# The S5 stage of a hybrid trunk kernel, put into a written order on all engines

## The chip, the cores and the metric

The kernel runs on one core of one Trainium2 chip. A core has TensorE (PE, with its weight loads PEld), VectorE (DVE), ScalarE (ACT), GpSimd (POOL) and SyncE (SP, which here only issues DMAs), each with a queue of its own that is worked off in order. The metric is the device time of one execution in microseconds (us), the median of several runs; lower is better.

## The reference

The input x has 512 tokens of 1024 channels, float32. Two layers follow each other; each is half a SwiGLU FFN (inner width 2816), a token mixer and another half FFN, all on RMS-normalised input with a residual. The first layer's mixer is a Mamba-2 SSD, the second's is an S5 diagonal state space model, and the change lies in that one:

```python
lam_bar = jnp.exp(lam * step)
b_bar = ((lam_bar - 1.0) / lam)[..., None] * lax.complex(b_re, b_im)
bu = jnp.einsum('bqgc,gpc->bqgp', uc.astype(jnp.complex64), b_bar)
...
_, states = lax.associative_scan(s5_binop, (a, bu), axis=1)   # state_t = lam_bar * state_(t-1) + bu_t
yc = jnp.einsum('gcp,bqgp->bqgc', c, states).real
...
y = jnp.moveaxis(ys, 0, 1).reshape(bsz, L, dm) + d * u
g = jax.nn.gelu(y)
val, gate = jnp.split(g @ glu_w + glu_b, 2, axis=-1)
return val * jax.nn.sigmoid(gate)
```

There are 64 groups of 16 channels with 64 complex states each. The GLU multiplies the 1024 channels by a 1024 x 2048 matrix.

## The kernel before, in words

The residual xT is held as eight tiles of 128 channels x 512 tokens. The kernel runs six stages: FFN, SSD, FFN, FFN, S5, FFN. Products are made with a high and a low half of each operand (three matmuls: hi x H, hi x L, lo x H; `proj`, lines 222 to 228). A weight tile is split by a cast on ACT (`whi`, line 217) and a subtraction on DVE (`wlo`, line 219). The FFN in front of S5 is `ffn7`; its last part writes the eight tiles of xT one after the other (line 587), stores each to DRAM as `d_u` (`s5_sink`, line 1289) and adds up the squares. A list `fill` of 62 small jobs is worked off beside it; jobs 54 to 61 come after the eight last columns.

**Layout of S5.** The 512 tokens are seen as 64 blocks of 8. u is read back from DRAM so that a partition holds one channel and one place in the block (`U`, 128 x 8 groups x 64 blocks, line 1316). Eight such tiles, i = 0 to 7, are worked on in pairs. For each i:

- U is multiplied by the norm factor rL (DVE, line 1368).
- 16 small matmuls with `opH` give the blocks' contributions to the states, `pb` (PE, line 1377).
- The scan over the 64 blocks, done in a turning frame so that the decay is real: two copies that swap the real and the imaginary half (ACT, lines 1380 and 1381), products with the table `tb` and their sum (DVE, lines 1382 to 1384), the scan itself (line 1386), two copies back (ACT, lines 1390 and 1391) and three DVE rows that turn the result into v (lines 1392 to 1394). The decay `rh` is laid out by POOL (lines 1370 and 1371).
- `mix`: for a pair and each half of its groups, eight matmuls on U and eight on v with `opP` (line 1404) and a gelu on ACT (line 1407).
- `channels`: transposes (line 1418) put a pair back into channels x tokens, and ACT and DVE split it into GH and GL (lines 1422 and 1423).
- `glu_k(k)`: the k-th of eight slices of the first four GLU column blocks (12 matmuls, lines 226 to 228). These four, `res`, have their weights split before the stage (lines 1346 and 1347). The fifth block, p0, gets 18 matmuls after glu_k(4) and glu_k(5), and six more after glu_k(7). The eleven others follow whole.

**The norm.** `compact_sum` (line 147) leaves the sum of squares of token t in a 128 x 4 layout, `newton_rsqrt` (lines 131 to 138) makes its inverse root in 13 small DVE rows, and lines 1355 to 1361 bring it into U's layout: a product with a mask, four matmuls with `sel` and a copy.

**What sets the order.** Under `manual_schedule(engines=MAN)` only PE keeps the order of the program text; a planner with a model of the times orders the other engines' work. Under `engines=ALL`, as inside `ffn7`, all five engines keep the order of the text. In before the S5 stage stands under MAN. Tiles come from pools with a fixed number of buffers: five for opH and tb together, five for opP, four for U, four PSUM banks for pb, mix and channels. A load into a buffer waits on SP until its last reader is done, and what SP has behind it waits too.

## Time and profile before

| | |
|---|---|
| median of 3 runs | 2068.3 us (2066.34 to 2068.41) |
| the profiled execution's own time | 2066.69 us |
| its span, first to last instruction | 2064.9 us |
| PE busy | 2005.0 us, 97% of the span |
| DVE, ACT, POOL busy | 1415.6, 890.3, 143.9 us |
| mean granted TensorE clock | 0.988 |

The S5 stage lies from about 1546 to 1706 us. In the profile's row of 40 slices for PE it is the one place (slice 31, from 1548.7 us) where the busy tenths fall to 5. An instruction's row in the timeline gives its start, its duration, engine, line, operation, tiles and shapes, "x" with the number of like instructions put together, and in brackets the idle time of the engine before it and what ended that. A float32 matmul counts as two (two passes), a split one as one.

### The profile page before, as it was taken

What the parts mean: (1) busy time and instruction counts of PE and PEld (TensorE: products, weight loads), DVE (VectorE), ACT (ScalarE), POOL (GpSimd) and SP (SyncE); (2) the same over time, 40 slices, a digit from 0 to 9 for tenths busy, and PEclk for the clock granted to TensorE, in tenths of its full rate; (3) what the DMA queues carried; (4) which work ended last, traced back from release to release, by engine and by line L of the source; (5) the groups of instructions that cost most, each with busy time, mean ns of one, the idle gap of its engine ahead of it and who ended that gap; (6) DMA issues with size and microseconds to landing.
All of it is one profiled execution on the core that took longest, in us unless ns stands there. A gap on an engine that the chain in (4) does not pass through costs nothing.

```text
span 2064.9 us, 30435 instructions
## 1 busy us (share of the span) xinstructions
PE 2005.0 (97%) x11905; PEld 1711.8 (83%) x11905; DVE 1415.6 (69%) x2494; ACT 890.3 (43%) x1454; POOL 143.9 (7%) x218
## 2 busy tenths in 40 slices
PE   8999999999999999999999999999995999999997
PEld 7888888878878877887788888999984888999996
DVE  6899445678875777557864567667667546866675
ACT  5322233556653674333433334444444433444553
POOL 1000000011110110000000000001111000100010
PEclk9999999999999999999999999999997999999999
DMA  6455643433334323535553325546769232755561
GB/s 168 113 147 161 173 112 86 117 113 100 108 106 110 107 69 112 160 101 160 153 142 97 94 84 142 125 120 149 176 169 303 90 94 67 178 127 119 129 143 67
DMA packets 422015, 262.85 MB, mean 127 GB/s; under 512 B 46600, under 2 KB 398512, under 8 KB 421616
## 3 DMA queue, kind: packets, MB, share of 16 engines
q1 hardware_dynamic: 383776, 205.81, 35.4%
q0 software_dynamic: 17808, 43.29, 9.0%
q10 hardware_dynamic: 20288, 11.81, 2.1%
q8 instruction: 93, 1.52, 0.3%
q14 instruction: 50, 0.41, 0.1%
HBM read 218.27 MB, written 24.25 MB: 117 GB/s over the span
## 4 chain that ended last, share of the span: by engine, by line
PE 59%; DVE 2%; DMA 1%; issue 1%; ACT 1%; ACTq 0%; DVEq 0%
PE mm L226 13%; PE mm L227 13%; PE mm L228 13%; PE mm L383 4%; PE mm L385 4%; PE mm L384 4%; PE aux L385 2%; PE aux L384 2%; PE aux L383 2%; DMA opH<-d_H 1%; PE aux L228 0%; PE aux L226 0%; PE aux L227 0%; PE aux L1404 0%; PE aux L1230 0%
## 5 line engine op out<-in xcount | busy, mean ns | idle before, releaser
L217 ACT CAST whi<-wst 128x1024 fp32r<-128x1024 f32 (+3 forms) x355 | 331.1, 933 | 573.6 <-PE mm L227 426.4
L226 PE MATMUL mm<-hH,whi 128*128 128x512 f32 x1256 | 496.1, 395 | 0.0
L227 PE MATMUL mm<-hL,whi 128*128 128x512 f32 x1256 | 491.2, 391 | 0.3 <-DVE hL L185 0.3
L228 PE MATMUL mm<-hH,wlo 128*128 128x512 f32 x1256 | 490.5, 391 | 0.0
L219 DVE TENSOR_TENSOR wlo<-wst,whi 128x1024 fp32r<-128x1024 f32 (+3 forms) x355 | 381.5, 1075 | 92.6 <-ACT whi L217 90.3
L226 PEld LDWEIGHTS mm<-hH,whi 128*128 128x128 f32 x1256 | 236.6, 188 | 50.8 <-issue 1.8
L228 PEld LDWEIGHTS mm<-hH,wlo 128*128 128x128 f32 x1256 | 236.3, 188 | 50.7 <-issue 0.6
L227 PEld LDWEIGHTS mm<-hL,whi 128*128 128x128 f32 x1256 | 236.7, 188 | 48.6 <-DVE hL L185 0.6
L227 PE MATMUL mm<-al,whi 128*128 128x512 f32 x704 | 274.6, 390 | 0.0
L228 PE MATMUL mm<-ah,wlo 128*128 128x512 f32 x704 | 274.3, 390 | 0.0
L226 PE MATMUL mm<-ah,whi 128*128 128x512 f32 x704 | 274.1, 391 | 0.0
L228 PEld LDWEIGHTS mm<-ah,wlo 128*128 128x128 f32 x704 | 132.2, 188 | 27.6 <-issue 0.2
L226 PEld LDWEIGHTS mm<-ah,whi 128*128 128x128 f32 x704 | 132.2, 188 | 27.2 <-issue 0.4
L227 PEld LDWEIGHTS mm<-al,whi 128*128 128x128 f32 x704 | 132.2, 188 | 26.9 <-issue 0.6
L383 PE MATMUL mm<-th,hH 128*128 128x256 f32 x408 | 115.7, 284 | 0.0
L385 PE MATMUL mm<-th,hL 128*128 128x256 f32 x408 | 115.4, 283 | 0.0
L384 PE MATMUL mm<-tl,hH 128*128 128x256 f32 x408 | 115.4, 283 | 0.0
L300 POOL DMA_DIRECT2D wu<-wst x34 | 28.8, 847 | 934.5 <-DMA wst<-in_ffn_w_in_dram 802.3
L264 DVE TENSOR_TENSOR up<-mm,rbc 128x512 f32<-128x512 f32 x43 | 29.7, 690 | 80.4 <-PE mm L228 80.0
L739 DVE SCALAR_TENSOR_TENSOR cv<-raw,cols,cv 128x512 f32<-128x512 f32 x96 | 76.2, 804 | 7.0 <-ACT cv L737 6.4
L383 PEld LDWEIGHTS mm<-th,hH 128*128 128x128 f32 x408 | 78.2, 192 | 1.6 <-ACT up L457 1.6
L587 DVE SCALAR_TENSOR_TENSOR xT<-mm,xT 128x512 f32<-128x512 f32 x80 | 54.9, 686 | 34.4 <-PE mm L228 34.3
(398 smaller groups left out, 3382.3 us busy)
## 6 DMA issues: line engine op xcount, KB each, us to landing
wst<-in_ffn_w_in_dram SPq DMA_DIRECT2D x142, 512.0 KB, 4.0
wst<-in_ssd_in_proj_dram SPq DMA_DIRECT2D x48, 512.0 KB, 3.9
wu<-in_ffn_w_in_dram SPq DMA_DIRECT2D x34, 512.0 KB, 6.0
wst<-in_ffn_w_out_dram SPq DMA_DIRECT2D x32, 448.0 KB, 3.8
wst<-in_ffn_w_out_dram SPq DMA_DIRECT2D x48, 256.0 KB, 2.9
wst<-in_ffn_w_out_dram SPq DMA_DIRECT2D x32, 320.0 KB, 3.2
wu<-wst POOLq DMA_DIRECT2D x34, 256.0 KB, 4.4
ws<-wst POOLq DMA_DIRECT2D x34, 256.0 KB, 5.3
```

Of the source, the lines that this page charges most:

```text
L217: S.copy(hi, st)
L219: V.tensor_tensor(lo, st, hi.bitcast(F32), op=OP.subtract)
L226: PE.matmul(ps, hi[:, k], H[k], start=first and k == 0, stop=False)
L227: PE.matmul(ps, hi[:, k], L[k], start=False, stop=False)
L228: PE.matmul(ps, lo[:, k], H[k], start=False, stop=last and k == n - 1)
L264: V.tensor_tensor(up, pu, pr.rbc, op=OP.mult)
L300: G.dma_start(dst, src, accum_op=OP.add)
L383: PE.matmul(ps[:, c0], hi[:, k], mh, start=first and k == 0, stop=False, skip_group_check=True)
L384: PE.matmul(ps[:, c0], hi[:, k], ml, start=False, stop=False, skip_group_check=True)
L385: PE.matmul(ps[:, c0], lo[:, k], mh, start=False, stop=k == 3, skip_group_check=True)
L587: V.scalar_tensor_tensor(xT[d], pos[d], 0.5, xT[d], op0=OP.mult, op1=OP.add)
L739: V.scalar_tensor_tensor(cv, raw[:, 1 + j:T + 1 + j], col("cw", j * 32 + ct), cv, op0=OP.mult, op1=OP.add)
```

## The change

- **Norm.** For S5 the squares are summed by 16 matmuls (eight on the running sum, eight on the last square) with sliding windows of a 128 x 136 tile `sel` that has ones in one column, so that the sum stands in U's layout, 128 x 64, at once. The Newton rows work on 128 x 64. The mask tiles, lines 1355 to 1361 and their matmuls go.
- **All engines in a written order** (`engines=ALL`) in the S5 stage. `scan` is taken apart into `decay`, `ur`, `states`, `swap`, `turn`, `scan`, `back` and `out`, `mix` into its part on U (w = 128) and its part on v (w = 0), and `gelu` stands by itself.
- **First pair in halves**: these steps of scans 0 and 1 work on four groups at a time (h0, h1).
- **Order**: the products on U stand ahead of the scans where the text puts them; in the loop over later pairs, states(i + 2) and glu_k(i - 2), glu_k(i - 1) stand ahead of the mixes of pair i.
- **Loads by need**: opP(0..1, 0..1), opP(2, 0), opH(2) and U(0..3) are loaded beside the last FFN columns; later opH, tb, opP and U each where the buffer comes free. The weights of `res` 2 and 3 are split in the stage, beside pair 2. The GLU columns from the fifth on are loaded (POOL) after pair 4's part of the loop and split at fixed places (`glu_load`, `glu_split`).

```diff
@@ -60,15 +60,7 @@
     make_identity(nc, ident)
     ones = const.tile([128, 128], F32, name="ones")
     V.memset(ones, 1.0)
-    kmask = const.tile([128, 64], F32, name="kmask")
-    half = const.tile([128, 2], F32, name="half")
-    const.tile([128, 16], F32, name="pad")
-
-    def masks():
-
-        V.tensor_reduce(kmask, ident.rearrange("p (e k) -> p k e", e=2), axis=AX.X, op=OP.add)
...
-    def newton_rsqrt(ps4, n, scale):
-
-        v = work.tile([128, 16], F32, name="nw_v")[:, :n]
-        hv = work.tile([128, 16], F32, name="nw_h")[:, :n]
-        y = work.tile([128, 16], F32, name="nw_y")[:, :n]
-        a = work.tile([128, 16], F32, name="nw_a")[:, :n]
+    def newton_rsqrt(ps4, n, scale, pool=None):
+
+        v, hv, y, a = [pool.tile([128, n], F32, name="nw5_" + nm, bufs=1) if pool else
+                       work.tile([128, 16], F32, name="nw_" + nm)[:, :n] for nm in "vhya"]
...
-            self.ps = compact_sum([self.acc, self.sq])
+            if self.kind != "s5":
+                self.ps = compact_sum([self.acc, self.sq])
+                return
+            self.ps = aux_ps()[:, 0:64]
+            for i, a in enumerate((self.acc, self.sq)):
+                for q in range(8):
+                    PE.matmul(self.ps, s5["sel"][:, 7 - q:135 - q], a[:, q * 64:q * 64 + 64], start=i == 0 and q == 0,
+                              stop=i == 1 and q == 7)
 
         def flush(self, keep=0):
             while len(self.later) > keep:
                 self.later.pop(0)()
 
         def finish(self):
+            if self.kind == "s5":
+                self.y4 = newton_rsqrt(self.ps, 64, 1.0 / D, s5["op"])
+                return
...
-    def in_ops(i):
+    def u_load(i):
 
         if i not in s5_in:
-            H = scan_ops(i, 1)[0]
             U = s5["op"].tile([128, 8, 64], F32, name="U", bufs=4)
             nc.sync.dma_start(U, s5["u"][i].rearrange("(g c) q k -> (c q) g k", c=16))
-            s5_in[i] = U, H, scan_ops(i, 2)[1]
+            s5_in[i] = U
...
-        st = res[j]
+    def res_hi(j):
+
         hi = [hpool.tile([128, 4, 128], F32R, tag="hH", name="hH") for _ in range(2)]
+        for i in range(2):
+            S.copy(hi[i], res[j][:, 4 * i:4 * i + 4])
+        res[j] = res[j], hi
+
+    def res_lo(j):
+
+        st, hi = res[j]
         lo = [hpool.tile([128, 4, 128], F32R, tag="hL", name="hL") for _ in range(2)]
         for i in range(2):
-            S.copy(hi[i], st[:, 4 * i:4 * i + 4])
             V.tensor_tensor(lo[i], st[:, 4 * i:4 * i + 4], hi[i].bitcast(F32), op=OP.subtract)
-        res[j] = (hi, lo)
+        res[j] = hi, lo
+
+    def res_w(j):
+        res_hi(j)
+        res_lo(j)
...
+            rL = pr.y4
+            def decay(i):
+
+                rh[i] = sp.tile([128, 8, 64], F32, name="rh", bufs=2)
+                G.memset(rh[i][:, :, 0:1], 0.0)
+                G.tensor_copy(rh[i][:, :, 1:], s5["rho"][:, gs8(i)][:, :, None].to_broadcast([128, 8, 63]))
+                vs[i] = sp.tile([128, 8, 64], F32, name="v1", bufs=3)
...
+            def ur(i, a=0, b=8):
+                U = u_load(i)
+                V.tensor_tensor(U[:, a:b], U[:, a:b], rL[:, None, :].to_broadcast([128, b - a, 64]), op=OP.mult)
...
+            def swap(i, a=0, b=8):
+                z2 = zs[i, a, 2] = sp.tile([128, 8, 64], F32, tag="z2", name="z2", bufs=3)[:, :b - a]
+                S.copy(z2[0:64], pbs[i][64:128, a:b])
+                S.copy(z2[64:128], pbs[i][0:64, a:b])
...
+            def mix(i, h, w):
+                if w:
+                    pys[i, h] = aux_ps()
+                py = pys[i, h]
+                for g in range(4):
+                    for e in range(2):
+                        PE.matmul(py[e * 64:e * 64 + 64, g * 128:g * 128 + 128],
+                                  (u_load(i + e) if w else vs[i + e])[:, h * 4 + g],
+                                  out_ops(i + e, h)[:, g, w:w + 128], start=bool(w) and g == 0,
+                                  stop=not w and g == 3, skip_group_check=True)
...
+            raw, wd = {}, {}
+
+            def glu_load(j):
+                if j < 2 * KD:
+                    raw[j] = fetch_w(glu_cols(j), KD, eng=G)[0]
+
+            def glu_split(j):
+                if j < 2 * KD:
+                    wd[j] = split_w(raw[j], KD)
+
+            h0, h1 = (0, 4), (4, 8)
+            for i in range(2):
+                decay(i)
+            ur(0, *h0)
+            ur(1, *h0)
+            states(0, *h0)
+            states(1, *h0)
+            mix(0, 0, 128)
+            ur(0, *h1)
+            ur(1, *h1)
+            states(0, *h1)
+            states(1, *h1)
+            mix(0, 1, 128)
+            scan_ops(2, 2)
+            scan_ops(3, 1)
+            swap(0, *h0)
+            turn(0, *h0)
+            swap(1, *h0)
+            scan(0, *h0)
+            back(0, *h0)
+            turn(1, *h0)
+            swap(0, *h1)
+            out(0, *h0)
+            scan(1, *h0)
+            back(1, *h0)
+            turn(0, *h1)
+            swap(1, *h1)
+            out(1, *h0)
+            mix(0, 0, 0)
+            gelu(0, 0)
+            ur(2)
+            ur(3)
+            decay(2)
+            states(2)
+            mix(2, 0, 128)
+            scan(0, *h1)
+            back(0, *h1)
+            turn(1, *h1)
+            out(0, *h1)
+            u_load(4)
+            scan_ops(3, 2)
+            out_ops(3, 0)
+            out_ops(2, 1)
+            states(3)
+            scan(1, *h1)
+            back(1, *h1)
+            swap(2)
+            turn(2)
+            out(1, *h1)
+            mix(0, 1, 0)
+            gelu(0, 1)
+            decay(3)
+            u_load(5)
+            out_ops(3, 1)
+            scan_ops(4, 1)
+            out_ops(4, 0)
+            res_hi(2)
+            res_hi(3)
+            mix(2, 1, 128)
+            scan(2)
+            back(2)
+            swap(3)
+            turn(3)
+            out(2)
+            lows = [channels(0, h) for h in range(2)]
+            for f in lows:
+                f()
+            res_lo(2)
+            res_lo(3)
+            scan_ops(4, 2)
+            for i in range(2, KD, 2):
+                nx = i + 2 < KD
+                scan(i + 1)
+                back(i + 1)
+                if nx:
+                    ur(i + 2)
+                    ur(i + 3)
+                    decay(i + 2)
+                    states(i + 2)
+                    scan_ops(i + 3, 1)
+                glu_k(i - 2)
+                glu_k(i - 1)
+                out(i + 1)
+                mix(i, 0, 0)
+                gelu(i, 0)
+                if nx:
+                    out_ops(i + 3, 0)
+                    out_ops(i + 2, 1)
+                    u_load(i + 4) if i + 4 < KD else None
+                    scan_ops(i + 3, 2)
+                mix(i, 1, 0)
+                gelu(i, 1)
+                if nx:
+                    out_ops(i + 3, 1)
+                    if i + 4 < KD:
+                        u_load(i + 5)
+                        scan_ops(i + 4, 1)
+                        out_ops(i + 4, 0)
+                    swap(i + 2)
+                    turn(i + 2)
+                    mix(i + 2, 0, 128)
+                    decay(i + 3)
+                    states(i + 3)
+                    scan(i + 2)
+                    back(i + 2)
+                    swap(i + 3)
+                    turn(i + 3)
+                    out(i + 2)
+                    lows = [channels(i, h) for h in range(2)]
+                    mix(i + 2, 1, 128)
+                    for f in lows:
+                        f()
+                    if i + 4 < KD:
+                        scan_ops(i + 4, 2)
+                if i == 4:
+                    for j in range(4, 8):
+                        glu_load(j)
+                if i == 6:
+                    glu_split(4)
+                    glu_split(5)
+                    glu_load(8)
+                    glu_load(9)
+            p0 = aux_ps()
             n0 = KD - 2
+            w0 = wd[4]
             proj(p0, [w_[:, :n0] for w_ in w0], GH[:n0], GL[:n0], last=False)
+            for f in [channels(KD - 2, h) for h in range(2)]:
+                f()
+            glu_split(6)
+            glu_load(10)
             for i in (KD - 2, KD - 1):
                 glu_k(i)
             proj(p0, [w_[:, n0:] for w_ in w0], GH[n0:], GL[n0:], first=False)
...
-                    proj(pp[-1], load_w(glu_cols(j), KD, eng=G), GH, GL)
+                    proj(pp[-1], wd[j], GH, GL)
+                    glu_split(j + 2)
+                    glu_load(j + 6)
...
-            with tc.manual_schedule(engines=MAN):
+            with tc.manual_schedule(engines=ALL):
...
-                    s5["sel"] = s5["op"].tile([128, 4, 16, 8], F32, name="sel", bufs=1)
+                    s5["sel"] = s5["op"].tile([128, 136], F32, name="sel", bufs=1)
                     G.memset(s5["sel"], 0.0)
-                    for t in range(4):
-                        G.tensor_copy(s5["sel"][:, t, :, 2 * t:2 * t + 2], half[:, None, :].to_broadcast([128, 16, 2]))
+                    G.memset(s5["sel"].rearrange("p (a b) -> p a b", b=8)[:, :, 7:8], 1.0)
+                    out_ops(0, 0)
+                    out_ops(1, 0)
 
                 fill = [lambda: None] * 62
                 fill[52] = lambda: (scan_ops(0, 2), scan_ops(1, 1))
                 fill[53] = lambda: scan_ops(1, 2)
-                fill[55] = lambda: res_load(0)
-                fill[56] = lambda: res_load(1)
-                fill[57] = lambda: (res_load(2), in_ops(0), res_w(0))
-                fill[58] = lambda: (res_load(3), in_ops(1))
-                fill[59] = lambda: res_w(1)
-                fill[60] = lambda: out_ops(0, 0)
-                fill[61] = lambda: (out_ops(1, 0), res_w(2))
+                fill[54] = lambda: out_ops(0, 1)
+                fill[55] = lambda: (res_load(0), out_ops(1, 1))
+                fill[56] = lambda: (res_load(1), scan_ops(2, 1))
+                fill[57] = lambda: (u_load(0), res_w(0))
+                fill[58] = lambda: (u_load(1), res_load(2))
+                fill[59] = lambda: (res_w(1), res_load(3))
+                fill[60] = lambda: u_load(2)
+                fill[61] = lambda: (u_load(3), out_ops(2, 0))
...
-                res_w(3)
```

More of the change, by code (lines that the diff above doesn't have):

```diff
@@ L62, in trunk_kernel @@
     V.memset(ones, 1.0)
-    kmask = const.tile([128, 64], F32, name="kmask")
-    half = const.tile([128, 2], F32, name="half")
-    const.tile([128, 16], F32, name="pad")
-    def masks():
-        V.tensor_reduce(kmask, ident.rearrange("p (e k) -> p k e", e=2), axis=AX.X, op=OP.add)
-        V.tensor_reduce(half, ident.rearrange("p (e k) -> p e k", e=2), axis=AX.X, op=OP.add)
+    const.tile([128, 24], F32, name="pad")
     xT = [const.tile([128, T], F32, name=f"xT{d}") for d in range(KD)]
@@ L1375, in scan, with states @@
+            def states(i, a=0, b=8):
+                U, W = u_load(i), scan_ops(i, 1)[0]
+                if i not in pbs:
+                    pbs[i] = aux_ps().rearrange("p (g k) -> p g k", g=8)
+                for g in range(a, b):
                     for hf in range(2):
                         m = slice(hf * 64, hf * 64 + 64)
-                        PE.matmul(pb[m, s], W[:, g, m], U[:, g], start=True, stop=True)
-                z1 = sp.tile([128, T], F32, name="z1", bufs=1)
-                z2 = sp.tile([128, 8, 64], F32, name="z2")
@@ L1444, in glu_out @@
                     xT[0] = s5["spare"]
-            ins = {}
-            for i in range(0, KD + 2, 2):
-                if i < KD:
-                    ins[i] = scan(i), scan(i + 1)
-                if i:
-                    gy = sp.tile([128, 8, 8, 16], F32, name="gy", bufs=1)
-                    mix(i - 2, ins[i - 2], gy)
-                if i >= 4:
-                    glu_k(i - 4)
-                    glu_k(i - 3)
-                if i:
-                    channels(i - 2, gy)
-            p0, w0 = aux_ps(), load_w(glu_cols(2 * NR), KD, eng=G)
+            raw, wd = {}, {}
```

104 lines of the change are left out of this document (47 added, 57 removed).

## The prediction

> **What bounds the kernel now.** I read the windows first: the profile cut at five points of the S5 stage (columns: window, its length, busy time of each engine, granted TensorE clock, DMA share, GB/s).
>
> ```profile
> 1546.10:1558.90 12.80, 2.74 (x74) 2.41 (x72) 8.56 (x24) 4.69 (x7) 4.27 (x8) 0.70 1.10 324
> 1558.90:1587.30 28.40, 12.43 (x200) 11.84 (x200) 21.46 (x32) 13.31 (x22) 3.93 (x9) 0.74 0.87 288
> 1587.30:1620.60 33.30, 29.92 (x338) 26.46 (x339) 27.86 (x42) 15.04 (x28) 2.97 (x12) 0.87 0.70 230
> 1620.60:1640.70 20.10, 20.08 (x126) 17.03 (x127) 4.74 (x10) 6.05 (x11) 0.00 (x0) 1.00 0.00 1
> 1640.70:1706.20 65.50, 65.28 (x287) 53.49 (x285) 36.70 (x42) 26.16 (x35) 4.41 (x5) 1.00 0.33 97
> ```
>
> TensorE is full outside this stretch and from 1620.6 on, so only its gaps from 1546 to 1620 can be won: 10.1 us while the norm is made, 16.0 us during the first pairs, 3.4 us after that. In the third window the eight scans run almost at VectorE's own pace (27.9 of 33.3 us). Whatever the new order does, the GLU's last matmuls follow the last scan. So I follow three marks: the end of scan 3 (fourth of eight), the end of scan 7, and the start of the first GLU projection after p0. Before, they stand at 1588.4, 1617.7 and 1640.7:
>
> ```profile
> 1587.15 1.22 DVE L1386 TENSOR_TENSOR_SCAN z<-rh,z 128x512 f32<-128x512 f32 x1
> ...
> 1616.50 1.22 DVE L1386 TENSOR_TENSOR_SCAN z<-rh,z 128x512 f32<-128x512 f32 x1
> ...
> 1640.72 0.39 PE L226 MATMUL aux<-gh,whi 128*128 128x512 f32 x1
> ```
>
> After the third mark both kernels have the same TensorE work and the same 65 us without a gap; a shift of the third mark is the change of the time.
>
> **The norm.** Before, y exists at 1555.2 and the scaled u starts at 1558.1, since splits stand between the Newton rows and a second matmul (L1359) follows:
>
> ```profile
> 1546.10 0.69 DVE L587 SCALAR_TENSOR_TENSOR xT<-mm,xT 128x512 f32<-128x512 f32 x1 [0.30 <-PE mm L228]
> 1549.26 0.15 DVE L131 TENSOR_SCALAR nw_v<-aux 128x4 f32<-128x4 f32 x1
> ...
> 1555.04 0.16 DVE L138 SCALAR_TENSOR_TENSOR nw_y<-nw_a,nw_y 128x4 f32<-128x4 f32 x1
> ...
> 1555.87 1.94 PE L1359 MATMUL aux<-rm,sel 128*128 128x64 f32 x8 [7.88 <-issue]
> 1557.85 0.22 DVE L1361 COPY rL<-aux 128x64 f32<-128x64 f32 x1 [2.18 <-PE aux L1359]
> ...
> 1617.58 1.03 PE L1418 MATMUL aux<-ident,gy 128*128 128x128 f32 x8
> 1618.54 1.09 PE L1404 MATMUL aux<-opP,U 128*64 128x128 f32 x16
> ```
>
> The new sums are 16 calls, 32 passes with 128-column weights. Eight such passes take 0.96 us at full clock (1617.58 to 1618.54) and 1.94 after a long gap (L1359). TensorE comes straight from the FFN, so I take 0.12 each: the acc half runs 1546.1 to 1548.0, the half on the last square until 1549.9. The 13 Newton rows become 64 wide: the 4-wide ones take 0.16, the 64-wide copy 0.22; with some 0.05 between dependent rows I take 0.26 each, 3.4 us, so y stands at **1553.3** (1552.5 to 1555.3: rows as now, or the second half of the sums at half clock). The removed mask reductions (at the kernel's start), the matmul and copy of L1359 to L1361, and sel's four POOL copies are on no path that is left.
>
> **The units.** Warm and cold prices of the stage:
>
> ```profile
> 1573.33 1.98 PE L1377 MATMUL aux<-U,opH 128*64 128x64 f32 x32 [10.24 <-DMA opH<-d_H]
> 1575.06 1.95 PE L1404 MATMUL aux<-opP,U 128*64 128x128 f32 x16
> 1576.76 1.95 PE L1404 MATMUL aux<-opP,v 128*64 128x128 f32 x16
> ...
> 1587.34 1.98 PE L1377 MATMUL aux<-U,opH 128*64 128x64 f32 x32 [3.78 <-issue]
> ...
> 1604.57 3.16 PE L1377 MATMUL aux<-U,opH 128*64 128x64 f32 x64 [2.15 <-DVE U L1368]
> 1607.45 1.98 PE L1404 MATMUL aux<-opP,U 128*64 128x128 f32 x16
> ...
> 1610.12 1.07 PE L1404 MATMUL aux<-opP,U 128*64 128x128 f32 x16
> 1611.00 1.07 PE L1404 MATMUL aux<-opP,v 128*64 128x128 f32 x16
> ...
> 1612.00 0.50 PE L226 MATMUL mm<-gh,hH 128*128 128x512 f32 x1
> ```
>
> States of one i: 1.44 warm (two from 1604.57 to 1607.45), 1.98 cold. One mix call (16 passes): 0.9 warm, 1.7 cold. Two glu_k: 5.5 (1612.00 to 1617.58). Both halves of channels: 1.0.
>
> ```profile
> 1608.01 0.69 DVE L1382 TENSOR_TENSOR z<-aux,tb 128x512 f32<-128x512 f32 x1 [0.77 <-ACT z L1381]
> 1608.62 0.68 DVE L1383 TENSOR_TENSOR z<-z,tb 128x512 f32<-128x512 f32 x1
> 1609.33 0.69 DVE L1384 TENSOR_TENSOR z<-z,z 128x512 f32<-128x512 f32 x1
> ...
> 1605.63 1.61 DVE L1423 TENSOR_TENSOR gl<-aux,gh 128x256 fp32r<-128x256 f32 x4
> ...
> 1542.46 1.29 DVE L1347 TENSOR_TENSOR hL<-wst,hH 128x512 fp32r<-128x512 f32 x2
> 1563.29 1.22 DVE L219 TENSOR_TENSOR wlo<-wst,whi 128x1024 fp32r<-128x1024 f32 x1
> ```
>
> A full VectorE row costs 0.6, 0.7 when it needs the row before; a half one (the gl width) 0.4.
>
> ```profile
> 1617.81 0.61 ACT L1390 COPY z<-z 64x504 f32<-64x504 f32 x1 [3.31 <-DVE z L1386]
> 1618.43 0.61 ACT L1391 COPY z<-z 64x504 f32<-64x504 f32 x1
> ...
> 1623.46 0.60 ACT L1407 ACTIVATE gy<-aux 128x512 f32<-128x512 f32 x1 [1.09 <-PE aux L1404]
> ...
> 1547.42 2.16 ACT L1346 CAST hH<-wst 128x512 fp32r<-128x512 f32 x4
> 1641.98 1.04 ACT L217 CAST whi<-wst 128x1024 fp32r<-128x1024 f32 x1
> ```
>
> A swap or a back is 1.2 on ScalarE, a gelu 0.6.
>
> **First pair, to scan 3.** Half units: u 0.4, states(0) first half 1.0 cold, swap 0.7, table product 0.4, sum 0.45, scan 0.7; then in the written VectorE order v 0.4, turn(1) 0.75, out(0) 0.85, sum and scan of 1 1.1, v 0.4, turn of the other half 0.75, out(1) 0.85: 8.8 us, so mix(0,0,0) starts at 1562.1 and ends at 1563.8. That frees the slot which opP(3,0) waits for; the load lands at the earliest 3.7 us later:
>
> ```profile
> L1324 SPq DMA_DIRECT2D opP<-d_P x16: 319/383/4182, 1549.8 to 1612.1; - x16
> DMA to landing us min/median/max: 3.7/6.8/15.3
> ```
>
> With 4.0, mix(2,0,128) runs 1567.8 to 1569.5. Queued behind it on TensorE: states(3) to 1571.2 and mix(0,1,0) to 1572.6. On ScalarE gelu(0,1) ends at 1573.2, the moved res_hi(2,3) at 1575.4, only then back(2) at 1576.6 and swap(3) at 1577.8. VectorE, waiting since 1574, then does the table product 0.65, out(2) 1.3, four gl 1.6, the moved res_lo 2.5, sum and scan 2.05: scan 3 ends at **1585.9**, 2.5 us before its old place. Without any wait the VectorE rows alone add up to 27 us from y (halves of scans 0 and 1 with their u 13.8, u(2,3) 1.2, scan 2 and its neighbours 6.3, gl and res_lo 4.0, scan 3 2.0): 1580.4.
>
> **The loop, where I expect the loss.** In before each pair of scans takes (1617.7-1588.4)/2 = 14.7 us. In the written loop, two glu_k stand between states(i+2) and the mixes of pair i, and swap(i+2) stands behind both gelus of pair i on ScalarE. So scan i+2, which needs only states and swap, waits for glu_k. From the end of scan i+1: v and u(i+2) 1.3; states(i+2) cold 2.0 (3.3); glu_k twice 5.5 and about 1.0 for its start at half clock (9.8); two mixes 1.8 (11.6); last gelu 0.65 (12.25); swap 1.2 (13.4); product, sum, scan 2.65 (16.1); back 1.2 (17.3); swap(i+3) 1.2 (18.5); product 0.65, out(i+2) 1.3, four gl 1.6 (22.0); sum and scan(i+3) 2.0: **24.0 us** per pair, 22.5 at full clock throughout. opP(i+3,0), freed at 10.7, lands at 14.7; mix and states(i+3) end at 17.1, just hidden under back(i+2). At the median 6.8 it isn't: +2.6. Two cycles put scan 7 at 1633.9: 48.0 against 29.3, a loss of 18.7. The u products ahead of the scans shorten none of these steps; of the 24 us TensorE has work for 13 (states 2.9, mixes 3.6, channels 1.0, glu_k 5.5).
>
> On the clock: after a gap of 3.78 us states took 1.98, after 2.15 us 1.44. [...]
>
> **The tail.** After: glu_k(4,5) start when the fourth gl is done, 2.0 before the end of scan 7, and end 3.5 after it; mixes 1.8 (5.3), gelu 0.65, then the moved split(4): cast 1.04 (7.0), wlo 1.2 (8.2). p0 stands behind it on TensorE, its 18 matmuls 4.1 less the few that need no wlo (12.0), channels 1.0, last gh and gl 1.0, glu_k(6,7) 5.5, last six of p0 1.4: 20.9 us. Before: 1640.7-1617.7 = 23.0. Gain 2.1. Splits and loads of the later columns get 5.5 us of TensorE per column as now; I cost them at nothing, and at 2.3 us (1.04+1.22) once if a column's cover is gone.
>
> **Moved loads.** Five opP and opH(2), by their shapes 3 MB, now go through SP's queue between the last FFN weights and the u stores:
>
> ```profile
> 1520.00:1540.00 20.00, 20.00 (x89) 16.53 (x89) 12.11 (x19) 8.03 (x13) 1.19 (x5) 1.00 0.53 153
> ```
>
> Over 26 us they add some 115 GB/s to 153, under the 324 of the window behind; I take nothing, and up to 3 us if a last weight tile comes late, with the split, the matmuls and the norm behind it. The GLU columns' loads stand on POOL behind decay(7), which gets its slot after mix(4,1,0), over 20 us ahead of split(4): nothing, as long as they don't slow opP.
>
> **Sum:** -2.5+18.7-2.1 = +14.1 us. The profiled execution took 2066.69 us around its span of 2064.9; the median of the runs, 2068.3, is 1.6 above it. Forecast 2066.7+14.1 = **2081**.
>
> **The rivals.**
> - *Queues pass each other* (faster): ScalarE takes swap(i+2) before the waiting gelu. Then a pair is the VectorE sum, 2x5.65+1.6+0.8 = 13.7, scan 7 ends at 1613.3, the third mark at 1634.2: -6.5, 2060. It decides wherever the first copy of scan 4's swap starts ahead of pair 2's gelus. For it: ScalarE is idle half of the stage, so nothing but the order holds the swap. Against: all engines are told to keep the order, and in the FFN before, which is written in the same way, squares wait 1.81 us for xT with a cast behind:
>
> ```profile
> 1546.88 0.63 ACT L170 ACTIVATE sq<-xT 128x512 f32<-128x512 f32 x1 [1.81 <-DVE xT L587]
> ```
>
>  Chance 0.08.
> - *The front pays more* (about the same): no wait before scan 3 (-5.5), cycles of 22.5 (-3.0), split(4) hidden (-2.9): +2.7, 2069. Against: each wait follows from a named predecessor. Chance 0.07.
> - *Landings at the median* (slower still): opP 6.8 instead of 4: front +2.8, two cycles +5.2, the sums' second half at half clock +2: 2091. For it: the row's median; against: that was taken with 288 GB/s in flight, the new loop needs by its tiles' shapes 4.5 MB in 24 us, 190 GB/s. Chance 0.15.
>
> **How the numbers follow.** Forecast 0.70, the rivals as above. A measurement of this kernel tells 0.2%, 4 us, from no change. Faster 0.08, within 0.2% 0.07, slower 0.85. The range goes from just under the second rival to the third: 2067 to 2092; only the first rival lies outside.
>
> **What would show it.** Right: the last Newton row near 1553, scan 3 ending near 1586, the next pairs 24 us apart; ScalarE idle ahead of both gelus of pairs 2 and 4 until TensorE's mixes, swap directly behind; two TensorE gaps a pair, the longer ended by a u product; a gap at p0 ended by wlo. Wrong: swap(4) ahead of gelu(2), scans 15 us apart, or a gap in the FFN's last columns.

## The result

The changed kernel takes **2095.28 us** (median of 4 runs, 2094.64 to 2098.06) against 2067.32 (4 runs, 2064.11 to 2068.41) for the kernel before on the same chip: ratio 1.014, 95% interval 1.0123 to 1.0158, 28 us slower. The forecast was 2081, the range 2067 to 2092: the sign was right, the loss is twice the forecast and the time lies outside the range. The profiled execution took 2095.54 us, its span is 2093.8.

These are the marks of the prediction in the timeline of after: the last column of xT, the first u product, scans 3 and 7, and the first projection after p0.

```profile
1548.68 0.68 DVE L587 SCALAR_TENSOR_TENSOR xT<-mm,xT 128x512 f32<-128x512 f32 x1
...
1555.92 1.43 DVE L1376 TENSOR_TENSOR U<-U,nw_y 128x256 f32<-128x256 f32 x4
...
1591.90 1.23 DVE L1404 TENSOR_TENSOR_SCAN z<-rh,z 128x512 f32<-128x512 f32 x1
...
1645.73 1.23 DVE L1404 TENSOR_TENSOR_SCAN z<-rh,z 128x512 f32<-128x512 f32 x1
...
1669.54 0.39 PE L226 MATMUL aux<-gh,whi 128*128 128x512 f32 x1
```

These are the windows of after, cut at these marks (same columns as in the prediction):

```profile
1548.68:1555.92 7.24, 3.76 (x32) 3.65 (x32) 3.43 (x15) 0.63 (x1) 0.60 (x2) 1.00 0.97 266
1555.92:1593.13 37.21, 18.68 (x232) 16.50 (x232) 26.37 (x53) 15.50 (x33) 2.94 (x9) 0.68 0.49 168
1593.13:1646.96 53.83, 36.01 (x326) 29.75 (x327) 26.35 (x40) 14.30 (x28) 7.26 (x13) 0.75 0.51 167
1646.96:1669.54 22.58, 19.51 (x108) 15.15 (x106) 7.51 (x11) 8.41 (x13) 2.65 (x3) 0.98 0.24 70
1669.54:1735.00 65.46, 65.26 (x287) 53.49 (x285) 38.49 (x43) 26.57 (x36) 4.41 (x5) 1.00 0.34 97
```

| stretch | before | after | difference | forecast |
|---|---|---|---|---|
| last xT starts | 1546.10 | 1548.68 | +2.6 | 0 |
| to the first u product | 12.0 | 7.2 | -4.8 | -4.8 |
| to the end of scan 3 | 30.3 | 37.2 | +6.9 | +2.3 |
| to the end of scan 7 | 29.3 | 53.8 | +24.5 | +18.7 |
| to the first projection after p0 | 23.0 | 22.6 | -0.4 | -2.1 |
| sum | | | +28.8 | +14.1 |

The last window is 65.5 us in both kernels with TensorE full, as the prediction had it, and from the third mark to the end of the span it is 424.2 us before and 424.3 after. The loop (third row of the windows) is where most of the time went: TensorE worked 36.0 of 53.8 us, VectorE 26.35, ScalarE 14.3. None of them is the bound; they wait for each other. The two waits that matter here, from 1593 to 1670 (us in total, times, longest):

```profile
ACT gy L1433 <- PE aux L1425: 27.3, 6, 11.1
DVE z L1395 <- ACT z L1390: 26.4, 4, 11.5
```

And this is the first cycle of the loop, row by row:

```profile
1593.76 1.69 DVE L1376 TENSOR_TENSOR U<-U,nw_y 128x512 f32<-128x512 f32 x2
...
1594.95 1.98 PE L1385 MATMUL aux<-U,opH 128*64 128x64 f32 x32 [8.24 <-issue]
1596.86 0.80 PE L226 MATMUL mm<-gh,hH 128*128 128x512 f32 x1
...
1604.08 1.97 PE L1425 MATMUL aux<-opP,v 128*64 128x128 f32 x32
...
1605.31 0.60 ACT L1433 ACTIVATE gy<-aux 128x512 f32<-128x512 f32 x1 [10.87 <-PE aux L1425]
1606.12 0.60 ACT L1433 ACTIVATE gy<-aux 128x512 f32<-128x512 f32 x1 [0.21 <-PE aux L1425]
1606.74 0.58 ACT L1389 COPY z<-aux 64x512 f32<-64x512 f32 x1
1607.34 0.58 ACT L1390 COPY z<-aux 64x512 f32<-64x512 f32 x1
...
1607.95 0.69 DVE L1395 TENSOR_TENSOR z<-aux,tb 128x512 f32<-128x512 f32 x1 [11.19 <-ACT z L1390]
```

The states of scan 4 stand ready at 1596.9. ScalarE is idle for 10.87 us up to the gelu of pair 2, because the two glu_k lie ahead of its mixes on TensorE (1596.86 to 1604.08), and the swap that scan 4 needs starts 9.8 us late, directly behind the second gelu; VectorE waits 11.19 us for it. This is the chain that the prediction named.

### The profile page after: what moved, and what is told of

Read it like the earlier page. It is cut to its first block, busy times and chain, and to the rows that moved or that the text cites. A ratio compares the mean times of both kernels' runs of the same rounds, so it can differ in the third digit from the quotient of the medians.

```text
span 2093.8 us, 30366 instructions
## 1 busy us (share of the span) xinstructions
PE 2018.1 (96%) x11865; PEld 1718.1 (82%) x11865; DVE 1419.2 (68%) x2506; ACT 890.1 (43%) x1462; POOL 143.8 (7%) x215
## 4 chain that ended last, share of the span: by engine, by line
PE 57%; DVE 2%; DMA 1%; issue 1%; ACT 1%; SPq 0%; POOL 0%; DVEq 0%; ACTq 0%
PE mm L226 13%; PE mm L227 13%; PE mm L228 12%; PE mm L383 4%; PE mm L385 4%; PE mm L384 4%; PE aux L385 2%; PE aux L384 2%; PE aux L383 2%; PE aux L1425 1%; DMA p_C<-d_C 0%; PE aux L228 0%; PE aux L1385 0%; DMA p_B<-d_B 0%; DMA opP<-d_P 0%
## 5 line engine op out<-in xcount | busy, mean ns | idle before, releaser
L300 POOL DMA_DIRECT2D wu<-wst x34 | 28.8, 847 | 933.9 <-PE mm L227 518.7
L384 PEld LDWEIGHTS mm<-tl,hH 128*128 128x128 f32 x408 | 78.3, 192 | 0.0
```

The source lines that it names most:

```text
L300: G.dma_start(dst, src, accum_op=OP.add)
L384: PE.matmul(ps[:, c0], hi[:, k], ml, start=False, stop=False, skip_group_check=True)
```

## The experiments

All kernels were timed beside the kernel before on the same chip; the ratio is to it. The median of before itself lay between 2064.8 and 2067.3 from chip to chip, so two experiments are compared by their distance to it (after: 28.0 us). "Step" is the time from the end of scan 3 to that of scan 5, and from 5 to 7, in the profile (after: 26.6 and 27.3; before: 14.7 on average). Theory A is that of the prediction: the order of the text, TensorE's and ScalarE's queues together.

**One edit of the loop at a time.** First the GLU products moved behind the mixes:

```diff
-                glu_k(i - 2)
-                glu_k(i - 1)
+                if not nx:
+                    glu_k(i - 2)
+                    glu_k(i - 1)
...
                     mix(i + 2, 1, 128)
+                    glu_k(i - 2)
+                    glu_k(i - 1)
```

> In the loop the two glu_k calls stand behind mix(i + 2, 1, 128) instead of ahead of the mixes of pair i (for the last pair they stay); all else as in the changed kernel. Theory A (TensorE's glu_k ahead of the mixes holds gelu, swap and so scan i + 2): the step from the end of one odd scan to the next falls from the 26.6 and 27.3 us of the changed kernel to about 19, with the gelus some 7 us earlier; glu_k(4,5) then start some 2 us later in the tail; time about 2095 - 13 = 2082 us. Rival B (the loads by need are the loss: TensorE's waits for opP): the opP waits stay, so the step stays near 26 and the time within 2 us of 2095.

Measured 2085.69 us, ratio 1.0101 (1.0086 to 1.0116); steps 20.0 and 19.7. The gelus start at 1601.00 and 1601.81, the wait ahead of them is 4.29 us where it was 10.87:

```profile
1594.17 1.22 DVE L1404 TENSOR_TENSOR_SCAN z<-rh,z 128x512 f32<-128x512 f32 x1
...
1601.00 0.60 ACT L1433 ACTIVATE gy<-aux 128x512 f32<-128x512 f32 x1 [4.29 <-PE aux L1425]
1601.81 0.60 ACT L1433 ACTIVATE gy<-aux 128x512 f32<-128x512 f32 x1 [0.22 <-PE aux L1425]
...
1614.17 1.23 DVE L1404 TENSOR_TENSOR_SCAN z<-rh,z 128x512 f32<-128x512 f32 x1
```

The distance to the kernel before falls from 28.0 to 20.9 us: a quarter of the loss is this one position. The two steps together are 14.2 us shorter, and not all of it arrives: from scan 7 to the first projection it takes 24.8 us instead of 22.6, since the last glu_k start later, and in this profile the norm's sums lost 2.8 us (see the last section). TensorE's waits for opP, the rival's cause, stayed what they were (5.5 us in the loop, 5.3 in after).

Second, only the swap moved:

```diff
                     states(i + 2)
+                    swap(i + 2)
                     scan_ops(i + 3, 1)
...
-                    swap(i + 2)
                     turn(i + 2)
```

> swap(i + 2) stands right behind states(i + 2), ahead of both gelus of pair i on ScalarE; TensorE's order, glu_k first, stays. Theory A (glu_k's place on TensorE carries the loss): scan i + 2 moves up by some 10 us, but back(i + 2) is still behind the gelus and states(i + 3) behind glu_k and the mixes, so the step is about 25 us instead of 27; time about 2092 us. Rival C (ScalarE's queue alone is the cause: the swap only had to pass the gelus): the step falls to 15 to 17 us and the time to about 2074.

Measured 2092.87 us, ratio 1.0134 (1.0119 to 1.0149); steps 25.45 and 25.2. Scan 4 now ends 8.4 us after scan 3 (row 1602.34 against 1593.89), but the gelus still come at 1606.61, back(4), swap(5) and scan 5 behind them:

```profile
1593.89 1.23 DVE L1404 TENSOR_TENSOR_SCAN z<-rh,z 128x512 f32<-128x512 f32 x1
...
1602.34 1.23 DVE L1404 TENSOR_TENSOR_SCAN z<-rh,z 128x512 f32<-128x512 f32 x1
1606.61 0.60 ACT L1433 ACTIVATE gy<-aux 128x512 f32<-128x512 f32 x1 [6.42 <-PE aux L1425]
...
1619.34 1.23 DVE L1404 TENSOR_TENSOR_SCAN z<-rh,z 128x512 f32<-128x512 f32 x1
```

The wait moved by half a pair and was paid there. The two steps are 3.2 us shorter, but the distance to the kernel before is 28.1 us, so no gain in the time can be told. ScalarE's queue alone is not the cause; it hands on what TensorE's order makes late. Third, both edits:

> Both edits: glu_k behind, swap(i + 2) ahead of the gelus. Theory A: the step is about 18.4 us, 0.8 under that of the first edit alone, since with the mixes early the gelus hardly hold the swap; time about 2080 us. Rival C (ScalarE's queue): nearly the same time as the swap edit alone, 2074, and the glu_k edit adds nothing. Rival B (opP): 2093.

Measured 2087.69 us, ratio 1.0112 (1.0092 to 1.0132), steps 20.9 and 20.7: a miss of the expectation (2080, steps of 18.4), and no gain over the first edit alone that can be told (four runs from 2083.9 to 2091.7). In the first cycle a new wait took over:

```profile
1600.02 0.95 SPq L1304 DMA_DIRECT2D tb<-d_t  x1
...
1607.29 0.69 DVE L1395 TENSOR_TENSOR z<-aux,tb 128x512 f32<-128x512 f32 x1 [5.90 <-DMA tb<-d_t]
```

The table of scan 5 is loaded "by need": it stands on SyncE's queue behind two opP loads that wait for the mixes' buffers, and it lands 7.3 us after its issue. In after this row waited for the swap alone. The next kernel has both edits, and the load moved ahead of those:

```diff
-                    scan_ops(i + 3, 1)
+                    scan_ops(i + 3, 2)
...
                     u_load(i + 4) if i + 4 < KD else None
-                    scan_ops(i + 3, 2)
```

> The kernel with both order edits (GLU products behind the second output mix, swap directly behind the states), and tb of the later step of the coming pair issued with its opH, ahead of the two opP loads and the U load in SyncE's queue instead of behind them. Theory A (what is left of the first step's 20.9 us is the 5.90 us wait of the z1 row for that tb): without it scan 5 is bound by its swap. From the trace with both edits: scan 4 ends 8.4 us after scan 3, back, swap, turn, out and the four gl rows follow, scan 5 ends 18.3 us after scan 3; the second step, whose z1 row waited for ScalarE and not for tb, stays at 20.7. 2.6 us less: 2085. Rival B (the opP loads take the wait over: pushed back in the queue by tb, they make mix(4,0,128), which stands ahead of states(5) on TensorE, wait longer): steps unchanged near 20.8, 2088.

Measured 2083.53 us, ratio 1.0089 (1.0074 to 1.0104); steps 18.1 and 17.5. The first step is as expected, the second better; the scans gain 6 us, of which 4 arrive. From scan 7 to the first projection it now takes 27.5 us (25.2 with the two edits alone): the GLU products that were put off stand there.

**The rivals in the loop.** In the next kernel the U part of the mix, which waits for an opP load, stands behind the states of the next scan:

```diff
-                    mix(i + 2, 0, 128)
                     decay(i + 3)
                     states(i + 3)
+                    mix(i + 2, 0, 128)
```

> mix(i + 2, 0, 128), which waits 2.6 us for opP(i + 3, 0), stands behind states(i + 3) instead of ahead of it. Theory A: swap(i + 3) waits for back(i + 2) anyway, the states come early for nothing, so the step stays at 26.5 to 27.3 us and the time at 2095 within 1 us. Rival B (the opP waits cost what they show): 2.6 us a pair, two pairs, time about 2090.

Measured 2096.56 us, ratio 1.0146 (1.0132 to 1.016), steps 26.0 and 26.9: no change. In the loop the opP landings, the mechanism of the prediction's third rival, are hidden under the other waits: they take 2.67 us of TensorE's idle time in a cycle, up to 1608.9, while back and swap are still to come. Another kernel has the text of after with a planner on all engines but TensorE:

```diff
-            with tc.manual_schedule(engines=ALL):
+            with tc.manual_schedule(engines=MAN):
                 s5_stage(pr, nxt)
```

> The S5 stage of the changed kernel with only TensorE kept in the written order; the planner orders the other four. It puts swap(i + 2) and back(i + 2) ahead of the gelus of pair i and spreads the splits, TensorE's order stays. Theory A: scan i + 2 comes early, but states(i + 3) stays behind glu_k, the mixes and an opP load, so the step is about 23 us and the time about 2087 us. Rival C (the written order off TensorE is the loss): the step falls to 15 us as in the kernel before, the time to 2070 or less.

Measured 2082.73 us, ratio 1.0085 (1.007 to 1.0101). This one is mixed: the planner mends one step (29.3, then 17.0), and xT(7) comes at 1554.58, 6 us later than in after. The loop still takes 46.3 us against 29.3 before, so freeing four queues doesn't by itself bring back the old pace. Why only the second step gained, with the GLU products ahead on TensorE in both, and what the planner did in the FFN's end, was not followed further.

**Ahead of the loop.** Rows on two queues show why xT comes late in after. The first is SyncE's queue:

```profile
1521.51 0.80 SPq L1323 DMA_DIRECT2D opP<-d_P  x2
1522.40 3.98 SPq L208 DMA_DIRECT2D wst<-in_ffn_w_out_dram  x4
```

The other is ScalarE's, where the cast of an FFN weight waits for its load:

```profile
1527.82 0.72 ACT L217 CAST whi<-wst 128x640 fp32r<-128x640 f32 x1 [7.11 <-DMA wst<-in_ffn_w_out_dram]
```

Two opP loads wait 16.9 us for memory that the FFN still uses (released by a VectorE row on `al`, L396), and the FFN's own output weights stand behind them; before, two of these were issued at 1516.47. In the next kernel those two loads stand later, beside opP(0,1):

```diff
-                    out_ops(0, 0)
-                    out_ops(1, 0)
...
-                fill[54] = lambda: out_ops(0, 1)
+                fill[54] = lambda: (out_ops(0, 0), out_ops(1, 0), out_ops(0, 1))
```

> opP(0, 0) and opP(1, 0) are issued after the FFN's first last column (job 54) instead of at the start of its last part; all else as in the changed kernel. Theory D (SP waits there for opP's memory to come free, and the last FFN weights, queued behind, come some 5 us late): the four weight loads go out near 1516.5 again instead of 1522.4, the weight cast of column 1 no longer waits for its load, xT(7) is written at 1546.1 instead of 1548.7, and the time falls by 2.6 us to about 2092.7. Rival E (the DMA engines are full): the FFN's end stays at 1548.7 or moves later, since the same bytes go out in a shorter stretch.

Measured 2096.19 us, ratio 1.0144 (1.0128 to 1.0159): a miss in the time. The first column is back (1524.37), but between the fourth and the fifth 7.0 us pass (1531.64 to 1538.64) instead of 4.0. On ScalarE the cast of the first GLU weight stands ahead of the cast for the fifth column, and its load, issued at 1527.44 behind three opP loads, landed 8.6 us later:

```profile
1536.04 1.14 ACT L1343 CAST hH<-wst 128x512 fp32r<-128x512 f32 x2 [2.99 <-DMA wst<-in_s_glu_w_dram]
```

The last xT still starts at 1546.75, 1.9 us sooner than in after. In the profile that gain is used up again: the norm's sums fell to half clock (granted 0.50 from 1549 on, rows of 2.67 and 3.62 us instead of 1.97 and 1.95), so that the first u product comes 9.6 us after the last xT instead of 7.2, and from scan 7 to the first projection it is 24.2 us instead of 22.6. So the time tells nothing about these loads, and the rows say that moving them only shifts the wait. The next kernel changes the half units of the first pair:

```diff
             mix(0, 0, 128)
+            swap(0, *h0)
+            turn(0, *h0)
+            swap(1, *h0)
             ur(0, *h1)
...
-            swap(0, *h0)
-            turn(0, *h0)
-            swap(1, *h0)
             scan(0, *h0)
```

> In the first pair, swap and turn of scan 0's first half and swap of scan 1's first half stand ahead of the second half's products and states; all else as in the changed kernel. Theory F (both halves of one scan lie in one PSUM tile, and the reads of the first half wait for the second half's matmuls, which the text puts ahead): the first swap starts about 1.5 us after the scaled u instead of 4.3, scan 3 ends some 2.5 us earlier after the scaled u (34.7 instead of 37.2), time about 2092.7. Rival G (the halves cost nothing, the first pair is held by its VectorE rows): the swap starts earlier, but scan 3 ends as before within 0.5 us.

Measured 2093.95 us, ratio 1.0135 (1.012 to 1.015). In after the first swap waits although its own half is done:

```profile
1560.26 0.37 ACT L1389 COPY z<-aux 64x256 f32<-64x256 f32 x1 [10.17 <-PE aux L1385]
```

Both halves of the states go into one PSUM tile, and the text of after puts the matmuls of the second half ahead of the copy, so it starts 4.3 us after the first u product. With the swap ahead of them it comes 1.65 us after it (1556.37 against 1554.72), the first scan 2.1 us earlier, and scan 3 ends 34.0 us after the u product instead of 37.2. The time shows nothing of it that can be told: the profiled execution was the fastest of four (2091.01 to 2097.42), and the median lies 28.0 us above the kernel before, as in after.

A like wait stands in the loop of after, where the z1 row of VectorE starts 0.03 us after the swap's second read of the same tile has ended (1607.92, 1607.95); in before it is 0.03 us too (1607.98, 1608.01). That the shared tile is the cause is the author's estimate: no run gives the two halves, or the two reads, tiles of their own. Then the norm alone, in the kernel before:

```diff
-            self.ps = compact_sum([self.acc, self.sq])
+            if self.kind != "s5":
+                self.ps = compact_sum([self.acc, self.sq])
+                return
+            self.ps = aux_ps()[:, 0:64]
...
-            rm = s5["op"].tile([128, 4, 64], F32, name="rm", bufs=1)
...
+            rL = pr.y4
```

> The kernel before with the norm part of the change alone: sums of squares and Newton rows in U's layout, no mask product, no second matmul; the stage's order stays the planner's. If the norm is worth what I worked out, the first product on u starts 3 to 5 us before 1558.1, and since the scans follow each other, the time falls by 2 to 5 us, to about 2063 beside 2067. If opH(3), which lands at 1573.3 behind the GLU weights, sets the first pairs, the gain stops there: within 1 us of before.

Measured 2064.79 us (11 runs), ratio 0.9994 (0.9985 to 1.0003): no difference that can be told. The first u product comes 9.55 us after the last xT instead of 12.0 (the planner puts rows of splits ahead of the Newton rows and among them), and scan 7 ends 68.9 us after it instead of 71.6. What of these 2.7 us reaches the end lies, by the interval, between 3.1 gained and 0.6 lost.

**All of it, and a version below both kernels.** The next kernel has the edits of the loop, the table ahead, the half units, the mix behind the states, and both last glu_k behind the gelus with the split of p0's weights behind out(7). Against the kernel with the table ahead, this part is new:

```diff
-                if not nx:
-                    glu_k(i - 2)
-                    glu_k(i - 1)
                 out(i + 1)
+                if not nx:
+                    glu_split(4)
                 mix(i, 0, 0)
...
                 if i == 6:
-                    glu_split(4)
+                    glu_k(4)
+                    glu_k(5)
                     glu_split(5)
```

> The previous kernel and three more moves: mix(i+2,0,128) behind states(i+3) on TensorE, the first half's swaps and turn ahead of the second half's states in the first pair, and in the last pair both glu_k behind the gelus with the split of the first projection's weights behind out(7). Theory A (written order throughout): steps 17 and 18 us instead of 20.9 and 20.7 (states(5) no longer waits for opP), first scans 3 us earlier, and about 3 us of TensorE gaps closed behind scan 7: 2087.7 - 6.6 - 2 - 3 = 2076. Rival G (with the waits gone TensorE's own work sets the pace, so what is gained in the loop is lost again behind it, where the products pile up): scan 7 ends some 10 us earlier than with both edits, but the first projection only 4 us earlier: 2083.

Measured 2077.40 us, ratio 1.0058 (1.0043 to 1.0073); steps 16.8 and 17.4, and 23.6 us from scan 7 to the first projection. That is near theory A's number (2076); rival G's (2083) is out. Then the loads of opP and opH(2) go back behind the FFN's weights, and the first mix on U behind the second half's states:

```diff
-            mix(0, 0, 128)
             swap(0, *h0)
...
             states(1, *h1)
+            mix(0, 0, 128)
             mix(0, 1, 128)
...
-                    out_ops(0, 0)
-                    out_ops(1, 0)
...
-                fill[54] = lambda: out_ops(0, 1)
-                fill[55] = lambda: (res_load(0), out_ops(1, 1))
-                fill[56] = lambda: (res_load(1), scan_ops(2, 1))
+                fill[55] = lambda: res_load(0)
+                fill[56] = lambda: res_load(1)
...
-                fill[60] = lambda: u_load(2)
-                fill[61] = lambda: (u_load(3), out_ops(2, 0))
+                fill[60] = lambda: (out_ops(0, 0), u_load(2))
+                fill[61] = lambda: (out_ops(1, 0), u_load(3), out_ops(0, 1), out_ops(1, 1), scan_ops(2, 1), out_ops(2, 0))
```

> As the previous kernel, with the loads of opP, opH(2) and the third and fourth resident weights' neighbours put back into the order of the kernel before: opP(0,0) and (1,0) at FFN jobs 60 and 61, opP(0,1), (1,1), (2,0) and opH(2) behind the last U load, so that nothing stands ahead of the FFN's output weights on SyncE's queue; mix(0,0,128) stands behind the second half's states. Theory A (the 2.6 us of the FFN's end are these loads' place in the queue): xT(7) near 1546.1 again, 2.6 us below the previous kernel, 2073 if that is at 2076. Rival E (the loads have to be somewhere: late, they hold the first mixes, which stand ahead of the next states on TensorE): xT(7) early, but the third scan no earlier, the same time as the previous kernel within 1 us.

Measured 2073.43 us, ratio 1.0037 (1.0023 to 1.0052). The last xT starts at 1544.98 (1548.74 in the kernel with the other edits). So the loads' place was the cause of the late FFN: with none of them ahead, no cast of its last columns waits for a load. Scan 3 ends 34.4 us after the first u product (34.7 in the kernel with the other edits), so the late loads don't hold the first scans, against rival E. Two more things moved in this profile: the sums ran at full clock (granted 1.00; 6.9 us from the last xT to the first u product instead of 9.5), and the second step grew from 17.4 to 20.8 us, because the two glu_k hold the states of scan 6 until 6.2 us after scan 5 (2.9 before this edit). At last the order was written once more, each move taken from a wait in the trace of the previous kernel (not shown below: glu_k(4) ahead of the last mixes, the last transposes ahead of p0's products, and the lines that only take part in the moves):

```diff
             swap(2)
+            res_hi(2)
+            res_hi(3)
             turn(2)
...
-            mix(2, 1, 128)
             scan(2)
             back(2)
             swap(3)
+            res_lo(2)
+            res_lo(3)
             turn(3)
-            out(2)
             lows = [channels(0, h) for h in range(2)]
+            mix(2, 1, 128)
...
+                out(i)
+                if nx:
+                    swap(i + 2)
...
-                    out(i + 2)
                     lows = [channels(i, h) for h in range(2)]
-                    mix(i + 2, 1, 128)
                     glu_k(i - 2)
                     glu_k(i - 1)
+                    mix(i + 2, 0, 128)
+                    mix(i + 2, 1, 128)
```

> The previous kernel (2073.4) with six more moves in the written order, each taken from a wait in its trace. First pair: the casts and subtractions of the third and fourth resident weights into idle stretches (behind swap(2) on ScalarE, behind scan(2) on VectorE) and the transposes of pair 0 ahead of mix(2,1,128). Loop: out(i+2) behind scan(i+3) and the next u products, transposes ahead of both mix(i+2,h,128), glu_k of the older pair directly behind the transposes. Last pair: glu_k(4) ahead of the mixes, the transposes ahead of the first projection's six products. Theory A (the order, and nothing in the hardware, costs the time): scan 3 ends 5.5 us earlier (2.2 of casts, 2.4 of subtractions, the rest gl rows), a pair takes 15.6 to 16 us instead of 16.8 and 20.8, and the tail 21 instead of about 25: 2073.4 - 5.5 - 5.7 - 3 = 2059, below the kernel before (2065). Rival G (TensorE's half clock in the loop sets the pair): scan 3 earlier by 5.5, pairs still near 19, the tail unchanged: 2068.

Measured **2059.83 us** (11 runs, 2058.79 to 2062.87) against 2065.00 (15 runs), ratio 0.9975 (0.9966 to 0.9984): 5.2 us below the kernel before, where after was 28.0 above it; steps 16.4 and 15.25. The windows of this kernel, cut at the same marks:

```profile
1546.28:1553.14 6.86, 3.67 (x32) 3.53 (x32) 3.43 (x15) 0.63 (x1) 1.33 (x6) 0.87 1.06 317
1553.14:1582.86 29.72, 17.22 (x232) 15.59 (x232) 25.33 (x51) 15.54 (x33) 2.94 (x9) 0.73 0.75 257
1582.86:1614.51 31.65, 27.68 (x304) 24.06 (x305) 26.27 (x40) 14.33 (x28) 7.24 (x13) 0.85 0.76 241
1614.51:1636.89 22.38, 20.93 (x134) 17.14 (x129) 8.70 (x13) 8.52 (x13) 2.65 (x3) 1.00 0.46 132
```

and its two waits in the place of those of after (from 1582 to 1637):

```profile
ACT gy L1433 <- PE aux L1425: 10.0, 6, 4.7
...
DVE z L1395 <- ACT z L1390: 4.5, 2, 2.7
```

The loop went from 53.8 to 31.7 us with the same instructions: VectorE's 26.3 and ScalarE's 14.3 us are the same to 0.1. TensorE's fell from 36.0 to 27.7, since it is less often at half clock (granted 0.85 instead of 0.75) and 22 matmuls now lie behind the mark. The two waits fell from 53.7 to 14.5 us. Against before, this loop is still 2.3 us longer: the written order did not beat the planner's there. The gain is the norm (12.0 to 6.9 us), with 0.5 of the first pair and 0.6 of the tail.

## Why the prediction was too low, and what of it was right

The forecast had the right mechanism for the largest part and came out at half the loss: 28.8 us in the profile, 14.1 foreseen. The 14.7 us between are four terms of its sum: the loop 5.8, the first pair 4.6, the moved loads 2.6, the tail 1.7.

- **What bounds it: right.** The three marks carried the whole difference; behind the third it is 424.2 us before, 424.3 after and 424.2 in the last kernel.
- **The norm: right, with some luck.** The first u product comes 4.8 us sooner after the last xT, as summed. But in six of nine profiles of kernels with this front the sums fell to half clock, and it came 1.7 to 2.8 us later than here. The prediction had that only as a bound and in its third rival.
- **The loop, mechanism: shown.** The forecast named glu_k ahead of the mixes on TensorE and the swap behind the gelus on ScalarE. Undoing the first took 7 us off the distance to the kernel before; the second alone took 3.2 us off the two steps and nothing off the time that can be told. A loop without either, with the further moves, comes to within 2.3 us of before.
- **The loop, size: 24.0 us foreseen, 26.6 and 27.3 measured.** The terms, from the end of scan 3 (1593.13): states end 3.8 after it (3.3 foreseen), glu_k 10.95 (9.8), mixes 12.9 (11.6), gelus 13.6 (12.25), swap 14.8 (13.4), scan 4 18.2 (16.1), swap 20.7 (18.5), scan 5 26.6 (24.0). The states end 0.5 later, the two glu_k are 0.65 longer than costed (7.2 instead of 6.5), and each half of the cycle loses 0.4 to 0.7 where the z1 row waits for the swap: the prediction let them run side by side, though before already has L1382 behind L1381 (0.03 us after its end). On the clock: after a gap of 8.24 us the states took 1.98 at a granted clock of 0.50 and the two glu_k 7.2 at 0.77. In before they took 1.44 at 0.74 and 5.5 at 1.00: 2.2 us less, where the prediction added 1.5 (24.0 against 22.5). No run shows the 1.0 of these 1.5 that was put on the start of the glu_k; in after it was 1.7.
- **The first pair: +6.9 instead of +2.3.** The step that failed is "states(0) first half 1.0 cold, swap 0.7" as a start of the chain: the swap does not begin at the first half's end, since the text puts the second half's matmuls into the same PSUM tile ahead of it. That is 2.9 of the 4.6 us (first copy 4.3 us after the u product instead of 1.4), and the kernel with the swap ahead won 3.2. The casts of res_hi ahead of back(2), then turn, gl and res_lo lie as foreseen: from the end of gelu(0,1) to that of scan 3 it is 12.8 us (12.7). The other 1.7 us lie between. The load of opP(3,0) is issued 3.3 us later than foreseen (1569.72, counted from the first u product), and it lands after 4.2 us, as reckoned (4.0). Another 1.0 comes between this landing and that gelu's end: TensorE worked there at a granted clock of 0.50 and took 5.8 us up to the gelu where 4.8 were foreseen.
- **Moved loads, costed at nothing: wrong by 2.6 us,** within the 3 us of the bound. The prediction reckoned the bytes, but the cost was a position: loads that wait for memory, ahead of the FFN's weights on one queue.
- **The tail: -0.4 instead of -2.1.** The term that failed is the end of glu_k(4,5), 3.5 us after scan 7, costed as warm: they run at half clock to 1648 (granted 0.50, 0.43 us from one to the next) and hold the mixes until 4.7 after it. The order behind them is as foreseen, the cast and wlo behind the gelus and p0 behind them:

```profile
1647.05 0.63 PE L226 MATMUL mm<-gh,hH 128*128 128x512 f32 x1
1647.48 0.63 PE L227 MATMUL mm<-gl,hH 128*128 128x512 f32 x1
...
1651.70 1.97 PE L1425 MATMUL aux<-opP,v 128*64 128x128 f32 x32
```

```profile
1655.28 2.36 DVE L219 TENSOR_TENSOR wlo<-wst,whi 128x1024 fp32r<-128x1024 f32 x2 [5.56 <-ACT whi L217]
```

- **The rivals.** ScalarE didn't pass the gelus: refuted by the order of its rows (the states of scan 4 stand ready at 1596.9, the gelus start at 1605.31 and 1606.12, the swap at 1606.74). The front won back nothing. Landings at the median were not the cause: the loads on which the sum leans landed 4.2 us (first pair) and 3.7 us (both cycles) after their issue, not 6.8. The measured time is 4 us above this third rival's, and this profile shows none of its reasons; one of them, the sums at half clock, shows in others.
- **The range** was too narrow because all four misses went one way, while its upper edge was taken from one rival.

## What to carry to other kernels

When a written order replaces a planner's, follow for each value that the next round needs every queue on which it stands, and put it ahead of all that the round doesn't need; here two GLU products ahead of a mix cost 14 us in the steps and 7 in the time, and a dozen moves of this kind made the difference between 28 us lost and 5 won. Undo one such place and the next wait takes over (the swap, then a load by need, then the tail), so judge an order by the whole chain and not by one edit. Count a load's place in the queue as its cost too: here two opP loads waited 16.9 us for a buffer ahead of the FFN's weights on one queue, and the last xT came 2.6 us later.

## What was not expected of the hardware

The same sums run at full or at half clock behind the same gap. These are after's rows, and those of the kernel with the GLU products behind, whose text is the same up to this point:

```profile
1548.97 1.97 PE L189 MATMUL aux<-acc,sel 128*128 128x64 f32 x16 [1.60 <-POOL v L1372]
1550.78 1.95 PE L189 MATMUL aux<-sq,sel 128*128 128x64 f32 x16
```

```profile
1548.77 3.11 PE L189 MATMUL aux<-acc,sel 128*128 128x64 f32 x16 [1.60 <-POOL v L1372]
1551.67 3.62 PE L189 MATMUL aux<-sq,sel 128*128 128x64 f32 x16
```

Both have 1.60 us of idle time ahead and a granted clock of 1.00 until then; the second kernel falls to 0.50 within the sums and loses 2.8 us there. Eight profiles show a gap of 1.54 to 1.63 us here: in three the sums ran at full clock (1.97 and 1.95 us), in five they fell (2.33 to 3.11 and 3.62). They fell in the kernel with the table ahead, too (3.6 for the second half). The two kernels with the loads behind the FFN have no gap at this place, and both ran the sums at full clock (1.97 and 1.95 us). So the profile of one execution can hold 2.8 us that another doesn't pay, and differences of this size between single profiles say little. Why the clock fell in the one and not in the other was not tried.
